# Attention in a fused two-layer trunk: both reciprocals of a unit stand behind the unit's last row minimum on VectorE, the normalisations on GpSimd follow them

## The chip, the cores and the metric

The kernel runs on one core of one Trainium2 chip. The metric is the device time of one launch in microseconds (us); lower is better. Engines are named as in the profile: PE is TensorE (PEld its weight loads), DVE is VectorE, ACT is ScalarE, POOL is GpSimd, SP is SyncE, whose queue issues the DMAs.

## The reference

Two layers over a sequence of 1024 tokens and width 1024, all in float32. Each layer has a token mixer and a SwiGLU feed-forward part, both normalised and modulated by a conditioning vector. Layer 0 mixes with forgetting attention (16 heads of 64), layer 1 with gated linear attention. The change touches the attention of layer 0 alone:

```python
proj = h @ w_in
q, k, v, f_logit = jnp.split(proj, [D_MODEL, 2 * D_MODEL, 3 * D_MODEL], axis=-1)
log_f = jax.nn.log_sigmoid(f_logit + b_f)
cum = jnp.cumsum(log_f, axis=1)
for blk in range(S // Q_BLOCK):                       # 8 blocks of 128 queries
    logits = einsum('bqhd,bkhd->bhqk', q[:, qs:qe], k[:, :qe]) * scale
    logits = logits + cum[:, :, qs:qe, None] - cum[:, :, None, :qe]
    p = softmax(where(causal mask, logits, -inf))
    outs.append(einsum('bhqk,bkhd->bqhd', p, v[:, :qe]))
return concatenate(outs) @ w_out
```

## The kernel before

Products are made in three matmuls of high and low parts, so that two 32-bit reduced operands give nearly a float32 result: `mm3` (lines 317, 318, 319) issues high by high, high by low, low by high. Every such operand has to be split first: ACT casts the high part, DVE or POOL subtracts it from the source (`split`, lines 175 and 176, and the same for weights at 243 and 247).

Attention goes by pairs of heads, `p` = 0 to 7, each with two heads `a`. A head has four units, `g`, worked on in the order 0, 3, 1, 2. A unit `(p, a, g)` is two rows of scores, `qi` = 0 and 1: query blocks `qb` = 2g and 2g+1, of (qb+1) x 128 keys. There are 64 units and 128 rows. For each row

- PE makes the scores in one or two tiles of up to 512 keys (tiles `s...`, lines 1348, 1350, and for some diagonal tiles a mask by 1352). The tiles take turns in two PSUM banks, b0 and b1, so a tile cannot be started before DVE has read the tile two before it.
- DVE takes the row minimum of the negated scores with the forgetting terms added (`tensor_tensor_reduce`, line 1356), from PSUM into the row's buffer `lp`. This is what frees the PSUM bank.
- ACT makes the exponential in place and its sum (line 1360).
- DVE makes the reciprocal of the sum, a 128x1 operation (line 1361).
- POOL multiplies the row by it in place (line 1362).

`outputs(u, lps)` then transposes the normalised rows on PE (tiles `t...`, line 1382, three PSUM banks), splits them on ACT and DVE into `pt`, multiplies them by the values on PE (tiles `o...`, lines 1394 and 1396, one PSUM bank), and adds the halves of that bank on ACT (1411) and DVE (1412) into `oT`. In the program it comes behind the scores of the next unit.

While the attention of pair p runs, PE also projects queries and keys for pair p+1 (tiles `qk...`) and values (tiles `vps...`); these take turns in two other PSUM banks, b6 and b7. A tile of queries is read by two ACT operations and then by two DVE operations of line 896 and 898 (`QA`, `QB`), 64x512 each. `weave` interleaves the two streams by estimated costs and lets the projections run ahead of the attention by at most 18 steps.

What stands on each engine's queue is settled when the kernel is built: a scheduler walks through the program with a timeline of its own estimates and puts, on each engine, the instruction that it takes to be ready. A queue is then strictly in order on the chip. `issue_after`, `in_order` and `behind_one` add constraints of order alone between instructions of one engine: `behind_one(e, at)` puts every instruction of engine `e` that is written in its block behind the instruction `at`, and `last_of(e)` is the last one written so far for `e`. In the program of before, the reciprocal and the normalisation of a row are written right behind its exponential, ahead of the next row's scores.

Of the kernel before, what the change touches and what calls it, by code (L numbers as in the profile page):

```python
# [14 lines left out]
ALU = mybir.AluOpType  # L15
# [3 lines left out]
D = 1024  # L19
# [34 lines left out]
def trunk(ctx, tc, x, c, ada_w, ada_b, norm1_g, norm2_g, ffn_w_in, ffn_w_out,  # L54
          fox_w_in, fox_b_f, fox_w_out, gla_w_in, gla_w_a2, gla_b_a, gla_g_o,
          gla_w_out, final_g, out, dbg=None, stop=None):
    nc = tc.nc
# [51 lines left out]
    def psl(t, n=1):  # L109
        return slice(t * P, (t + n) * P)  # L110
# [145 lines left out]
    @contextmanager  # L256
    def behind_one(e, at):

        bb = nc.cur_bb.bb.instructions
        n = len(bb)  # L260
        yield
        for i in bb[n:]:
            if i.engine == ENG[e]:
                tc.add_manual_dep(i, at.name, mybir.DependencyInfo(
                    mybir.DependencyClass.NoSync, mybir.DependencyReason.DATA), reason="order")
# [36 lines left out]
    class Weights:  # L302
# [7 lines left out]
        def next(self):  # L310
            while self.loads and len(self.got) < self.depth:
                f, *a = self.loads.popleft()
                self.got.append(f(*a))
            return self.got.popleft()
# [133 lines left out]
    def last_of(e):  # L448
        return next(i for i in reversed(nc.cur_bb.bb.instructions) if i.engine == ENG[e])
# [877 lines left out]
    def scores(u):  # L1327

        p, a, g = u
        t = qkt[p]  # L1330
        Qs, K1, KL = (t["QA"], t["KA"], t["KLA"]) if a == 0 else (t["QB"], t["KB"], t["KLB"])
        cm = cums[2 * p + a]
        own = {0: near_t[:, 0:P], 1: near_t[:, P:], 4: far_t[:, 0:2 * P], 5: far_t[:, 2 * P:]}
        if g < 2:
            both = lpr([P, (4 * g + 3) * P], F32, f"lp{p}{a}{g}")
            lps = [both[:, 0:(2 * g + 1) * P], both[:, (2 * g + 1) * P:]]
        else:
            lps = [lpr([P, (2 * g + 1 + i) * P], F32, f"lp{p}{a}{g}{i}") for i in range(2)]
        st = sm.tile([P, 2, 4], F32, tag="st", bufs=4, name=f"st{p}{a}{g}")
        for qi in range(2):  # L1340
            qb = 2 * g + qi
            qs, lp, Wd, mcur = psl(qb), lps[qi], (qb + 1) * P, 3e38
            cuts = (0, 384, 640) if Wd == 640 else (0, Wd) if Wd <= HALF else (0, HALF, Wd)
            for n_, (k0, k1) in enumerate(zip(cuts, cuts[1:])):
                ps = sr([P, k1 - k0], F32, f"s{p}{a}{qb}{k0}")
                early = u == (0, 0, 0)
                diag = k1 == Wd
                nc.tensor.matmul(ps, Qs[:, qs], K1[:, k0:k1], start=True, stop=False)
                by_pe = diag and qb in (2, 3, 6)
                nc.tensor.matmul(ps, Qs[:, qs], KL[:, k0:k1], start=False, stop=not by_pe)  # L1350
                if by_pe:
                    nc.tensor.matmul(ps[:, k1 - k0 - P:], identb, maskb, start=False, stop=True)
                mnew = st[:, qi, n_:n_ + 1]
                cmk = own[qb] if diag and qb in own else cm[:, k0:k1]
                with tc.issue_after(v_last) if early else ExitStack():
                    nc.vector.tensor_tensor_reduce(lp[:, k0:k1], ps, cmk, 1.0, mcur,  # L1356
                                                   ALU.add, ALU.min, mnew)
                mcur = mnew
                yield max(0.22, 0.00085 * (k1 - k0))
            nc.scalar.activation(lp, lp, AF.Exp, bias=mcur, scale=-1.0, accum_out=st[:, qi, 2:3])  # L1360
            nc.vector.reciprocal(st[:, qi, 3:4], st[:, qi, 2:3])  # L1361
            nc.gpsimd.tensor_scalar(lp, lp, st[:, qi, 3:4], 1.0, op0=ALU.mult, op1=ALU.mult)  # L1362
        return lps

    def outputs(u, lps):
# [60 lines left out]
    def attention(p):  # L1426
        for a in range(2):
            h = 2 * p + a
            for i, g in enumerate(ORDER):
                u = (p, a, g)  # L1430
                if h and i == 1:
                    mask_far()
                lps = yield from scores(u)
                if i == 0:
                    if h:
                        mask_last(h)
                    load_near(h + 1)
                elif i == 1:
                    mask_near(h + 1)
                elif i == 3:  # L1440
                    load_far(h + 1)
                    load_cum(h + 2)
                if p:
                    if p > 0:
                        ada0(0.4)
                    ada0p(0.8)
                if pending[0] is not None:
                    yield from finish(*pending[0])
                pending[0] = (u, lps)
        if p == 7:  # L1450
            yield from finish(*pending[0])
# [1197 lines left out]
```

## Time and profile before

| | |
|---|---|
| three runs | 2345.64 us median, 2344.7 to 2349.95 |
| the profiled execution | 2345.56 us, of which the span of the core's work is 2343.8 |
| attention | about 98 to 592 us of the span |
| PE busy | 2322.6 us, 99% of the span |
| DVE, POOL, ACT busy | 1772.7 us (76%), 1160.5 us (50%), 1128.0 us (48%) |
| L1361, reciprocals | 128, 163 ns each |
| L1362, normalisations | 128, 775 ns each in the mean |
| mean granted TensorE clock | 0.997 |

PE is the busiest engine by far. But a matmul's busy time covers its latency, and a following one overlaps it: matmuls of 512 columns that follow each other start about 0.23 us apart and last 0.39 us each. So a stall of less than some 0.15 us is not seen as idle time, and a longer one is seen shortened by about that. Starts of matmuls, one after the other, tell more than the busy share.

### The profile page before, as it was taken

The page shows a single profiled execution, that of the slowest core. Times are in us where ns is not written, and L with a number is a line of the kernel's source. Part 1 is how long each engine was busy: PE and PEld are TensorE (multiplying, and loading weights), DVE is VectorE, ACT ScalarE, POOL GpSimd, SP SyncE. Part 2 cuts the span into 40 slices and gives each one's busy share as a digit, 9 for nine tenths or more (in the row PEclk, how much of TensorE's full clock was granted, in tenths as well). Part 3 has the DMA queues.
Part 4 walks back from the last instruction along what each step waited for, and adds up shares of the span by engine and source line. Part 5 has one row for each costly group of instructions (what it writes and reads, how often), then busy time and mean ns, then how long its engine had stood idle before and what let it go on. Part 6 is the DMA issues. An engine that isn't in the chain of part 4 may idle for free.

```text
span 2343.8 us, 35552 instructions
## 1 busy us (share of the span) xinstructions
PE 2322.6 (99%) x12088; PEld 1980.6 (85%) x12088; DVE 1772.7 (76%) x2946; ACT 1128.0 (48%) x2166; POOL 1160.5 (50%) x1027
## 2 busy tenths in 40 slices
PE   8999999999999999999999999999999999999999
PEld 7988888888888888788888899898888888888888
DVE  6577677776788888997888666668787777876787
ACT  6566566675544333334325654345444333345236
POOL 1345454533446656665563522345456666664651
PEclk9999999999999999999999999999999999999999
DMA  8533343352435545459774443555434544458674
GB/s 259 163 99 112 109 120 107 113 169 84 153 100 175 187 158 176 154 203 315 267 265 155 136 128 99 151 171 172 150 102 162 174 147 159 141 189 300 237 264 141
DMA packets 359342, 390.72 MB, mean 167 GB/s; under 512 B 26908, under 2 KB 296376, under 8 KB 359160
## 3 DMA queue, kind: packets, MB, share of 16 engines
q1 hardware_dynamic: 359160, 388.45, 50.7%
q8 instruction: 95, 1.56, 0.3%
q14 instruction: 87, 0.71, 0.1%
HBM read 287.10 MB, written 101.25 MB: 166 GB/s over the span
## 4 chain that ended last, share of the span: by engine, by line
PE 54%; DVE 4%; DMA 3%; POOL 2%; issue 2%; SPq 0%; ACT 0%; POOLq 0%; DVEq 0%; ACTq 0%
PE p_b L317 11%; PE p_b L319 11%; PE p_b L318 11%; PE gv_b L317 1%; PE gv_b L319 1%; PE gv_b L318 1%; PE gr_b L317 1%; PE gr_b L319 1%; PE gr_b L318 1%; DVE o_s L176 1%; DVE ad_s L543 1%; DMA ex_s<-x_sp 1%; PE gqp_b L317 0%; PE gk_b L317 0%; PE f1a_b L319 0%
## 5 line engine op out<-in xcount | busy, mean ns | idle before, releaser
L175 ACT CAST o_s<-xv_s 128x512 fp32r<-128x512 f32 (+1 forms) x392 | 235.9, 610 | 328.4 <-PE p_b L319 218.5
L176 DVE TENSOR_TENSOR o_s<-xv_s,o_s 128x512 fp32r<-128x512 f32 (+1 forms) x392 | 332.7, 854 | 37.2 <-ACT o_s L175 36.3
L317 PE MATMUL p_b<-B,o_s 128*128 128x512 f32 x608 | 235.4, 391 | 0.9 <-DVE ex_s L1745 0.5
L318 PE MATMUL p_b<-B,o_s 128*128 128x512 f32 x608 | 236.1, 389 | 0.0
L319 PE MATMUL p_b<-B,o_s 128*128 128x512 f32 x608 | 235.1, 389 | 0.0
L978 POOL TENSOR_TENSOR ex_s<-xv_s,xv_s 128x512 f32<-128x512 f32 (+1 forms) x64 | 96.0, 1499 | 238.8 <-DMA xv_s<-in_ffn_w_in_dram 123.3
L1362 POOL TENSOR_SCALAR lp_s<-lp_s,st 128x128 f32<-128x128 f32 (+7 forms) x128 | 98.9, 775 | 220.9 <-DVE st L1361 191.8
L317 PE MATMUL p_b<-T,o_s 128*128 128x512 f32 x480 | 186.7, 390 | 1.8 <-DVE x L1745 1.8
L318 PE MATMUL p_b<-T,o_s 128*128 128x512 f32 x480 | 186.7, 389 | 0.0
L319 PE MATMUL p_b<-T,o_s 128*128 128x512 f32 x480 | 181.2, 389 | 0.0
L1360 ACT ACTIVATE lp_s<-lp_s,st 128x128 f32<-128x128 f32 (+7 forms) x128 | 99.5, 777 | 85.4 <-DVE st L1356 68.1
L317 PEld LDWEIGHTS p_b<-B,o_s 128*128 128x128 f32 x608 | 114.1, 188 | 26.6 <-issue 1.6
L319 PEld LDWEIGHTS p_b<-B,o_s 128*128 128x128 f32 x608 | 114.1, 188 | 23.9
L318 PEld LDWEIGHTS p_b<-B,o_s 128*128 128x128 f32 x608 | 114.2, 188 | 23.2
L980 POOL TENSOR_TENSOR xv_s<-ex_s,xv_s 128x512 f32<-128x512 f32 (+1 forms) x64 | 95.7, 1495 | 51.2 <-DVE o_s L176 47.9
L1745 DVE TENSOR_TENSOR ex_s<-ex_s,p_b 128x512 f32<-128x512 f32 x140 | 94.2, 680 | 29.9 <-PE p_b L319 29.6
L990 POOL TENSOR_TENSOR xv_s<-xv_s,xv_s 128x512 f32<-128x512 f32 x48 | 65.8, 1370 | 97.9 <-issue 54.7
L176 DVE TENSOR_TENSOR pt_s<-t_b,pt_s 128x512 fp32r<-128x512 f32 (+1 forms) x160 | 98.4, 632 | 20.3 <-ACT pt_s L175 19.1
L317 PEld LDWEIGHTS p_b<-T,o_s 128*128 128x128 f32 x480 | 90.1, 188 | 21.3 <-DVE x L1745 2.2
L175 ACT CAST pt_s<-t_b 128x512 fp32r<-128x512 f32 (+1 forms) x160 | 82.6, 544 | 51.1 <-PE t_b L1382 32.6
L319 PEld LDWEIGHTS p_b<-T,o_s 128*128 128x128 f32 x480 | 90.1, 188 | 18.7
L318 PEld LDWEIGHTS p_b<-T,o_s 128*128 128x128 f32 x480 | 90.1, 188 | 18.6
(1539 smaller groups left out, 7378.2 us busy)
## 6 DMA issues: line engine op xcount, KB each, us to landing
xv_s<-in_ffn_w_in_dram SPq DMA_DIRECT2D x176, 256.0 KB, 3.2
hid_B<-x SPq DMA_DIRECT2D x66, 512.0 KB, 3.0
ad_s<-in_ada_w_dram SPq DMA_DIRECT2D x384, 64.0 KB, 2.4
hid_T<-x SPq DMA_DIRECT2D x44, 512.0 KB, 2.9
xv_s<-in_ffn_w_out_dram SPq DMA_DIRECT2D x88, 256.0 KB, 3.6
T2o<-hid_T SPq DMA_DIRECT2D x22, 512.0 KB, 7.0
T1o<-hid_T SPq DMA_DIRECT2D x22, 512.0 KB, 6.2
B11o<-hid_B SPq DMA_DIRECT2D x22, 512.0 KB, 5.9
```

Of the source, the lines that this page charges most:

```text
L175: nc.scalar.copy(hi, src)
L176: nc.vector.tensor_sub(lo, src, hi.bitcast(F32))
L317: nc.tensor.matmul(ps, ah, bh, start=start, stop=False, skip_group_check=chain)
L318: nc.tensor.matmul(ps, ah, bl, start=False, stop=False, skip_group_check=chain)
L319: nc.tensor.matmul(ps, al, bh, start=False, stop=stop, skip_group_check=chain)
L543: nc.vector.scalar_tensor_tensor(acc, raw[:, t], c42[:, o:o + 1], acc, op0=ALU.mult, op1=ALU.add)
L978: nc.gpsimd.tensor_add(s1, a21, a22)
L980: nc.gpsimd.tensor_sub(a11, s1, a11)
L990: nc.gpsimd.tensor_sub(r[A12], r[A12], r[A11])
L1360: nc.scalar.activation(lp, lp, AF.Exp, bias=mcur, scale=-1.0, accum_out=st[:, qi, 2:3])
L1362: nc.gpsimd.tensor_scalar(lp, lp, st[:, qi, 3:4], 1.0, op0=ALU.mult, op1=ALU.mult)
L1745: nc.vector.tensor_add(d, d if src is None else dest(G, src), ps)
```

## The change

The reciprocals and the normalisations of both rows are written behind the loop over the rows, that is behind the exponential of the second row, and the reciprocals are held on DVE behind the last row minimum of the unit.

```diff
             nc.scalar.activation(lp, lp, AF.Exp, bias=mcur, scale=-1.0, accum_out=st[:, qi, 2:3])
-            nc.vector.reciprocal(st[:, qi, 3:4], st[:, qi, 2:3])
-            nc.gpsimd.tensor_scalar(lp, lp, st[:, qi, 3:4], 1.0, op0=ALU.mult, op1=ALU.mult)
+        at = last_of("D")
+        for qi in range(2):
+            with behind_one("D", at):
+                nc.vector.reciprocal(st[:, qi, 3:4], st[:, qi, 2:3])
+            nc.gpsimd.tensor_scalar(lps[qi], lps[qi], st[:, qi, 3:4], 1.0, op0=ALU.mult, op1=ALU.mult)
         return lps
```

Every instruction is kept, none is added. Lines behind the change move by three (1361 becomes 1364, 1362 becomes 1365, 1382 becomes 1385, 1396 becomes 1399). Because the scheduler settles all queues anew, the order within attention changes on every engine, on PE too; from the end of attention on all queues stand as before. In the rows below a name carries p, a, and then g for a row buffer (`lp2030`: p 2, a 0, g 3, row 0) or qb and the first key for a score tile (`s207512`: p 2, a 0, qb 7, keys from 512); `b0` or `b1` behind it is the PSUM bank.

PE in the unit (2, 0, 3) and the next one, where the profile of before has its longest waits. Before:

```order
L1348 MATMUL s207512_b1_54_2582<-KA2_1686,QA2_1684 128x512
L1350 MATMUL s207512_b1_54_2582<-KLA_201,QA2_1684 128x512
L1382 MATMUL t2000_b3_41_2606<-ident_67,lp200_s48_28_2451 128x128 x3
L1348 MATMUL s2020_b0_55_2627<-KA2_1686,QA2_1684 128x384
L1350 MATMUL s2020_b0_55_2627<-KLA_201,QA2_1684 128x384
L1352 LDWEIGHTS identb_72
L1352 MATMUL s2020_b0_55_2627<-maskb_84,identb_72 128x128
L1348 MATMUL s2030_b1_56_2638<-KA2_1686,QA2_1684 128x512
L1350 MATMUL s2030_b1_56_2638<-KLA_201,QA2_1684 128x512
L1352 LDWEIGHTS identb_72
L1352 MATMUL s2030_b1_56_2638<-maskb_84,identb_72 128x128
L1348 MATMUL s2040_b0_57_2763<-KA2_1686,QA2_1684 128x384
```

The same place of the program on PE after the change:

```order
L1348 MATMUL s2070_b0_53_2576<-KA2_1686,QA2_1684 128x512
L1350 MATMUL s2070_b0_53_2576<-KLA_201,QA2_1684 128x512
L319 MATMUL qk031_b7_18_2571<-h0h7_189,w384_l_s24_18_1936 128x512
L317 MATMUL vps20_b6_19_2708<-wv2560_0h_s19_19_2193,h0h0_175 128x256
L318 MATMUL vps20_b6_19_2708<-wv2560_0l_s20_20_2194,h0h0_175 128x256
L319 MATMUL vps20_b6_19_2708<-wv2560_0h_s19_19_2193,h0l0_176 128x256
L317 MATMUL vps20_b6_19_2708<-wv2560_0h_s19_19_2193,h0h1_177 128x256
L318 MATMUL vps20_b6_19_2708<-wv2560_0l_s20_20_2194,h0h1_177 128x256
L319 MATMUL vps20_b6_19_2708<-wv2560_0h_s19_19_2193,h0l1_178 128x256
L1348 MATMUL s207512_b1_54_2580<-KA2_1686,QA2_1684 128x512
L1350 MATMUL s207512_b1_54_2580<-KLA_201,QA2_1684 128x512
L1399 MATMUL o112_b5_16_2494<-pt1120_s50_38_2500,v00_s27_1_797 128x256 x4
```

Before, five score tiles stood in a row with three transposes between them; after, each is set apart by projections or products with the values (`s2020` comes ten rows behind the last row shown, `s2030` much later).

PE in the unit (5, 0, 3). Before:

```order
L1348 MATMUL s5070_b0_125_4879<-KA5_3990,QA5_3988 128x512
L1350 MATMUL s5070_b0_125_4879<-KLA_201,QA5_3988 128x512
L319 MATMUL vps32_b7_38_5015<-wv2816_0h_s19_43_4489,h0l1_178 128x256
L1396 MATMUL o412_b5_40_4795<-pt4120_s50_98_4801,v20_s27_9_2829 128x256
L1348 MATMUL s507512_b1_126_4883<-KA5_3990,QA5_3988 128x512
L1350 MATMUL s507512_b1_126_4883<-KLA_201,QA5_3988 128x512
L1396 MATMUL o412_b5_40_4795<-pt4120_s50_98_4801,v20_s27_9_2829 128x256 x3
L1396 MATMUL o412_b5_40_4795<-pt4121_s51_99_4812,v21_s28_10_2953 128x256
L1382 MATMUL t5000_b3_101_4902<-ident_67,lp500_s48_64_4747 128x128 x3
L317 MATMUL vps32_b7_38_5015<-wv2816_0h_s19_43_4489,h0h2_179 128x256
```

The same place on PE after the change; ahead of these rows stand, from the last matmul of the query tile `qk061` on, three matmuls of `vps32`, the two of `s506512`, eight of `o411`, the mask of `s506512` and one matmul of `vps32`:

```order
L1348 MATMUL s5070_b0_125_4877<-KA5_3990,QA5_3988 128x512
L1350 MATMUL s5070_b0_125_4877<-KLA_201,QA5_3988 128x512
L318 MATMUL vps32_b7_38_5015<-wv2816_0l_s20_44_4490,h0h1_177 128x256
L319 MATMUL vps32_b7_38_5015<-wv2816_0h_s19_43_4489,h0l1_178 128x256
L1385 MATMUL t5000_b3_101_4902<-ident_67,lp500_s48_64_4747 128x128 x3
L1348 MATMUL s507512_b1_126_4881<-KA5_3990,QA5_3988 128x512
L1350 MATMUL s507512_b1_126_4881<-KLA_201,QA5_3988 128x512
L1348 MATMUL s5020_b0_127_4923<-KA5_3990,QA5_3988 128x384
L1350 MATMUL s5020_b0_127_4923<-KLA_201,QA5_3988 128x384
L1352 LDWEIGHTS identb_72
L1352 MATMUL s5020_b0_127_4923<-maskb_84,identb_72 128x128
L1399 MATMUL o412_b5_40_4795<-pt4120_s50_98_4801,v20_s27_9_2829 128x256 x4
```

Here the score tile `s5020`, which needs the bank of `s5070`, has moved up to stand right behind `s507512`, and `o412` behind it.

DVE at that place, from the minimum of `s506512` on. Before:

```order
L1356 ISA lp5030_s45_65_4853,st503_4855<-s506512_b1_124_4863,cum10_s43_11_4330,st503_4855 128x384
L1356 ISA st503_4855 128x1
L176 TENSOR_TENSOR pt4120_s50_98_4801<-t4120_b3_98_4796,pt4120_s50_98_4801 128x512
L176 TENSOR_TENSOR pt4121_s51_99_4812<-t4121_b4_99_4807,pt4121_s51_99_4812 128x512
L176 TENSOR_TENSOR pt4122_s49_100_4822<-t4122_b2_100_4818,pt4122_s49_100_4822 128x384
L1356 ISA lp5031_s46_66_4854,st503_4855<-s5070_b0_125_4879,cum10_s43_11_4330 128x512
L1356 ISA st503_4855 128x1
L1361 RECIPROCAL st503_4855<-st503_4855 128x1
L1356 ISA lp5031_s46_66_4854,st503_4855<-s507512_b1_126_4883,cum10_s43_11_4330,st503_4855 128x512
L1356 ISA st503_4855 128x1
L247 TENSOR_TENSOR w1792_l_s24_48_4998<-w1792__s16_43_4995,w1792_h_s23_47_4997 128x256
L896 SCALAR_TENSOR_TENSOR QA6_4753<-qk061_b6_37_4872,QA6_4753 64x512
```

After:

```order
L1356 ISA lp5030_s45_65_4853,st503_4855<-s506512_b1_124_4863,cum10_s43_11_4330,st503_4855 128x384
L1356 ISA st503_4855 128x1
L896 SCALAR_TENSOR_TENSOR QA6_4753<-qk061_b6_37_4872,QA6_4753 64x512
L898 SCALAR_TENSOR_TENSOR QB6_4754<-qk061_b6_37_4872,QB6_4754 64x512
L1356 ISA lp5031_s46_66_4854,st503_4855<-s5070_b0_125_4877,cum10_s43_11_4330 128x512
L1356 ISA st503_4855 128x1
L176 TENSOR_TENSOR pt4121_s51_99_4812<-t4121_b4_99_4807,pt4121_s51_99_4812 128x512
L1415 TENSOR_TENSOR oT4_s52_5_4129<-o411_b5_39_4721,oT4_s52_5_4129 64x256
L176 TENSOR_TENSOR pt4122_s49_100_4822<-t4122_b2_100_4818,pt4122_s49_100_4822 128x384
L1356 ISA lp5031_s46_66_4854,st503_4855<-s507512_b1_126_4881,cum10_s43_11_4330,st503_4855 128x512
L1356 ISA st503_4855 128x1
L1364 RECIPROCAL st503_4855<-st503_4855 128x1
```

The reciprocal of the first row (L1361, now L1364) has gone from between the minima of `s5070` and `s507512` to behind the latter, as the change asks in every unit; and the reading of the query tile (`QA6`, `QB6`) has come to stand ahead of the minimum of `s5070`.

## The prediction

> **What bounds the kernel now.** I read the page first, then the sums by stage, then PE's waits in attention, then the timeline at each place where PE waited.
>
> ```profile
> span 2343.8 us, 35552 instructions
> 220.00:280.00 60.00, 58.28 (x379) 51.68 (x379) 40.63 (x111) 38.24 (x82) 32.60 (x48) 0.97 0.36 109
> 280.00:340.00 60.00, 58.91 (x395) 52.87 (x394) 44.38 (x116) 38.12 (x81) 31.04 (x44) 1.00 0.35 108
> 592.00:800.00 208.00, 207.96 (x943) 172.69 (x942) 170.66 (x234) 93.92 (x159) 111.79 (x79) 1.00 0.48 156
> ```
>
> The columns of a stage are its length, then busy time (and count) of PE, PEld, DVE, ACT and POOL, the granted clock, and the DMA. PE is busy for nearly all of every stage, DVE for two thirds of it. So DVE is not the bound, and the change can only be worth what PE loses inside attention, 98 to 592 us. The stage behind attention has no idle PE (207.96 of 208 us) and an unchanged order: what attention gains or loses arrives at the end in full.
>
> ```profile
> PE s_b L1348 <- DVE st L1356: 1.5, 2, 1.2
> PE t_b L1382 <- POOL lp_s L1362: 1.0, 1, 1.0
> ...
> PE mp_b L460 <- DVE QB L898: 0.6, 1, 0.6
> ```
>
> ```profile
>   ACT lp_s L1360: 31.6, 50
> ...
>   POOL lp_s L1362: 191.8, 78
> ```
>
> The first fence is PE's waits within attention (total, times, longest): a score tile waited for a row minimum, a transpose for a normalisation, each once or twice. The second is the reciprocal of line 1361: DVE stood 31.6 us, in 50 waits, for the exponential, and POOL stood 191.8 us for DVE. Large numbers, but hardly any of it reaches PE.
>
> The places where it does, in order of time: place A, PE and DVE, unit (2, 0, 3) and the next.
>
> ```profile
> 231.31 0.49 PE L1382 MATMUL t_b<-ident,lp_s 128*128 128x128 f32 x3
> 231.91 0.44 PE L1348 MATMUL s_b<-KA,QA 128*128 128x384 f32 x1
> 232.11 0.74 DVE L1356 CUSTOM_DVE_ANT_0 lp_s<-s_b,cum_s,st 128x512 f32<-128x512 f32 x1
> 232.37 0.23 PE L1352 MATMUL s_b<-maskb,identb 128*128 128x128 bf16 x1
> 232.89 0.68 DVE L896 SCALAR_TENSOR_TENSOR QA<-qk_b,QA 64x512 fp32r<-64x512 f32 x1
> 232.92 0.50 PE L1348 MATMUL s_b<-KA,QA 128*128 128x512 f32 x1 [0.32 <-DVE st L1356]
> 233.49 0.23 PE L1352 MATMUL s_b<-maskb,identb 128*128 128x128 bf16 x1
> 233.59 0.69 DVE L898 SCALAR_TENSOR_TENSOR QB<-qk_b,QB 64x512 fp32r<-64x512 f32 x1
> 234.31 0.56 DVE L1356 CUSTOM_DVE_ANT_0 lp_s<-s_b,cum_s 128x384 f32<-128x384 f32 x1
> 234.93 0.44 PE L1348 MATMUL s_b<-KA,QA 128*128 128x384 f32 x1 [1.21 <-DVE st L1356]
> 235.22 0.34 PE L1350 MATMUL s_b<-KLA,QA 128*128 128x384 f32 x1
> 235.63 0.38 PE L1382 MATMUL t_b<-ident,lp_s 128*128 128x128 f32 x1
> 236.00 2.29 PE L1396 MATMUL o_b<-pt_s,v_s 128*128 128x256 f32 x9
> ```
>
> ```profile
> 235.00:236.00 1.00, 0.92 (x4) 0.37 (x4) 0.94 (x3) 0.68 (x2) 0.35 (x1) 0.87 0.95 337
> 236.00:239.00 3.00, 3.00 (x15) 3.00 (x15) 2.47 (x9) 1.19 (x3) 1.69 (x2) 0.50 0.01 2
> 239.00:240.00 1.00, 1.00 (x10) 1.00 (x10) 0.00 (x0) 0.00 (x0) 1.00 (x3) 0.93 0.00 0
> ```
>
> Place B, a few units later (PE, and QB on DVE):
>
> ```profile
> 295.67 0.40 PE L1350 MATMUL s_b<-KLA,QA 128*128 128x512 f32 x1
> 295.92 0.69 DVE L898 SCALAR_TENSOR_TENSOR QB<-qk_b,QB 64x512 fp32r<-64x512 f32 x1
> 296.67 0.61 PE L460 MATMUL mp_b<-four,acc_s 128*128 128x4 f32 x4 [0.60 <-DVE QB L898]
> ...
> 297.86 0.23 PE L1352 MATMUL s_b<-maskb,identb 128*128 128x128 bf16 x1
> ...
> 298.46 0.74 PE L1396 MATMUL o_b<-pt_s,v_s 128*128 128x256 f32 x4 [0.37 <-DVE oT_s L1412]
> ```
>
> Rows for pricing the new order, from the place called E below as it ran before, and from a reciprocal that waited and its normalisation:
>
> ```profile
> 415.33 0.62 DVE L1356 CUSTOM_DVE_ANT_0 lp_s<-s_b,cum_s,st 128x384 f32<-128x384 f32 x1
> 417.14 0.40 PE L1350 MATMUL s_b<-KLA,QA 128*128 128x512 f32 x1
> 417.37 0.28 PE L319 MATMUL vps_b<-wv_0h_s,h0l 128*128 128x256 f32 x1
> 417.49 0.28 PE L1396 MATMUL o_b<-pt_s,v_s 128*128 128x256 f32 x1
> 417.61 0.40 PE L1348 MATMUL s_b<-KA,QA 128*128 128x512 f32 x1
> 417.68 0.69 DVE L1356 CUSTOM_DVE_ANT_0 lp_s<-s_b,cum_s 128x512 f32<-128x512 f32 x1
> ...
> 228.85 0.69 DVE L176 TENSOR_TENSOR pt_s<-t_b,pt_s 128x512 fp32r<-128x512 f32 x1
> ...
> 414.87 0.43 DVE L1412 TENSOR_TENSOR oT_s<-o_b,oT_s 64x256 f32<-64x256 f32 x1 [0.40 <-ACT oT_s L1411]
> ...
> 230.40 0.16 DVE L1361 RECIPROCAL st<-st 128x1 f32<-128x1 f32 x1 [0.86 <-ACT lp_s L1360]
> ...
> 230.90 1.01 POOL L1362 TENSOR_SCALAR lp_s<-lp_s,st 128x896 f32<-128x896 f32 x1
> ```
>
> From start to start, matmuls of 512 columns take 0.23 us (417.14 to 417.37) and of 256 columns 0.12; I take 0.18 for 384 between these, and 0.11 for a transpose (three in 0.49, of which one latency). Those are PE's real costs; the longer durations overlap.
>
> **The change part by part.** No instruction comes or goes, so no engine's work changes. Three things move.
>
> *DVE's waits for the exponential.* The first row's reciprocal now stands behind the second row's minima, when its exponential is long done. I cost this at nothing by itself: PE's list has no wait that ends on line 1361. The second row's reciprocal still has to wait for the exponential that follows the last minimum. Behind a waiting reciprocal on DVE stand minima and splits; they get earlier, and that is cover for what comes below.
>
> *The first row's normalisation and transposes.* Reciprocal and POOL's multiplication start behind the last minimum instead of behind the first row's exponential. On POOL's queue the multiplication falls behind weight splits and adaLN products that stood after it; no wait of PE ends on those. On SP no transfer belongs to the moved step; loads of the forgetting terms wait for row minima, which do not get later by it, and no matmul in attention waits for a load. PE's order follows: the first row's transposes stand later too. From the last score matmul to the first transpose the new queue has 2.3 us of PE work at the closest unit, (7, 1, 3), and 3.7 at the next. Needed are: latency and start 0.25, minimum 0.69, its accumulator 0.08, reciprocal 0.16, 0.34 from its end to POOL's start (230.56 to 230.90), multiplication 1.01: 2.5 us. So 0.3 us of wait at one unit, and cover of over 1 us at all others: **+0.3**.
>
> *PE's order of score tiles.* A score tile needs the bank of the tile two before it. PE work between that tile's last matmul and this one's first, summed over the queue by the costs above, is the cover for the minimum. Before, the five shortest of 190 are 0.6 to 1.1 us (`s2040`, `s706512`, `s2030`, `s2020`, `s307512`); a minimum alone takes 0.25 + 0.7. After, none is under 1.2.
>
> Place A goes. Its waits, start to start less the cost: 0.27 at `s2020` (231.31 to 231.91), 0.49 at `s2030` (mask at 232.37, next 232.92, 0.06 for the mask), 1.38 at `s2040` (233.49 to 234.93), 0.23 and 0.26 at the two steps behind (235.22 to 235.63 to 236.00), since DVE's backlog reached the splits: 2.6 us. And the granted clock fell to 0.50 behind it: 1 us at 0.87, 3 at 0.50, 1 at 0.93 lose 0.13 + 1.5 + 0.07 = 1.7 us. Together **-4.3**. In the new queue these three have 3.4 to 3.7 us of PE work as cover, against 0.6 to 1.0.
>
> Place B goes as well: in the new queue the `mp` product comes some 60 rows later, `s3020` has projections ahead of it, and `o212` stands far from `o211`. Its cost: 0.77 (295.67 to 296.67, less 0.23) + 0.37 at `s3020` + 0.54 (297.86 to 298.46, less 0.06) = 1.7. The middle one is the rest of the same backlog, taken at the size of its neighbour's shown idle time. **-1.7**.
>
> Place E is new: unit (5, 0, 3). Count from the start of the last `qk061` matmul. PE: 0.23, three `vps` 0.36, `s506512` 0.36, eight `o411` 0.95, mask: its result stands at about 2.1. DVE: minimum of `s506512` 0.62 + 0.08 to 2.8; QA and QB, which now stand ahead, 0.68 + 0.69 to 4.15; minimum of `s5070` 0.69 to 4.85. PE meanwhile: mask and `vps` to 2.05, `s5070` 0.46, `vps` 0.24, transposes 0.33, `s507512` 0.46: at 3.5 it stands before `s5020`, which needs the bank of `s5070`: a wait of 1.4. Then `s5020` and its mask, 0.45, and `o412` at 5.35 needs the one `o` bank, freed by oT of `o411`, which on DVE stands behind a split: 4.93 + 0.69 + 0.43 = 6.05: a wait of 0.7. **+2.1**. It is place A's pattern on a smaller scale: QA and QB in front of a minimum.
>
> Waits that I leave as they are: those around 468, 485 and 500 to 520 us, where the new order is nearly the old.
>
> Sum: -4.3 - 1.7 + 2.1 + 0.3 = -3.6 us, on the profiled execution's 2345.56 (span 2343.8 and 1.8 around it; 0.08 under the median of the runs, 2345.64): **2342.0 us**, 0.15% faster. What a measurement of this kernel tells from no change is about 0.2%, 4.7 us, so the forecast counts as the same.
>
> [...]
>
> **The rivals.**
>
> *E does not bite, and the gain is larger.* If ACT and DVE run ahead at E by what the reciprocals no longer hold up (one wait cost DVE 0.86), the minimum of `s5070` is in time. For it: the 31.6 us of such waits; against: what delays it is work, not a wait. Then -4.3 - 1.7 + 0.3 = -5.7: 2339.9, faster by 0.24%.
>
> *The clock drops at E.* Its 2.1 us of waits within 2.6 us are close to A's 2.6 within 4.5. Then +1.7: 2343.7, the same.
>
> *Slower: POOL comes late for the first row.* In the new queue the closest seven units have 2.3, 3.7, 4.1, 4.1, 4.2, 4.4 and 4.6 us of PE work ahead of the first transposes. If POOL is busy with other rows when the reciprocal is done, so that the chain takes 5.1 us rather than 2.5, PE waits 2.8 + 1.4 + 1.0 + 1.0 + 0.9 + 0.7 + 0.5 = 8.3, of which 0.3 is counted: 2342.0 + 8.0 = 2350.0. It decides from a chain of about 4.5 on. For it: before, PE did wait for POOL once, 1.0 us. Against: POOL is half idle.
>
> *Nothing reaches PE.* A and B go, but other bunches of like size that I have not seen come: 2345.6. For it: the waits are set by a scheduler that knew nothing of them; against: the distances, of which the shortest have grown.
>
> **How the numbers follow.** Forecast 0.36; E harmless 0.31; clock drop at E 0.17; other bunches 0.09; POOL late 0.07. Faster by over 0.2%: the second case and nothing else, 0.31. Slower: POOL late, and 0.01 of the bunches, 0.08. Same: 0.61. The range of 8 in 10 reaches from E harmless with 0.5 us of small waits gone, 2339.4, to the clock drop with about 1.5 more of bunches, 2345.2.
>
> **What the profile will show.** Right: no wait of PE for line 1356 around 231 to 235 us and no stage at 0.97 clock there; the wait for `mp` gone; one wait of PE of over 1 us for a minimum near 415 us with QA and QB ahead of it on DVE; DVE's wait for the exponential about halved from 31.6. Wrong: a clock under 1.00 in 400 to 460; new waits of PE for POOL's line 1365; a gain spread over all of attention rather than at two places.

## The result, and the profile after

The changed kernel took 2342.72 us (median of 12 runs, 2338.45 to 2346.55), the kernel before 2345.97 in the runs beside them (12, 2344.35 to 2351.16). The ratio is 0.9981, with a 95% interval of 0.9973 to 0.9989: 0.19% faster. That is 4.5 us, the difference of the means; the medians are 3.25 us apart. It is clear of no change, and just under the 0.2% from which the prediction counts a kernel as faster. The forecast was 2342.0. One run of the experiment e2 below took 8960.03 us and is left out of its ratio, not of its median; all other runs of this study took 2334 to 2353 us. The profiled execution took 2340.03 us, its span is 2338.3.

The stages of the changed kernel that answer to those of before (columns as there), and PE's waits within attention:

```profile
220.00:280.00 60.00, 60.00 (x401) 53.74 (x400) 44.14 (x116) 38.76 (x84) 33.87 (x49) 1.00 0.36 112
280.00:340.00 60.00, 59.90 (x399) 53.75 (x398) 44.86 (x120) 38.48 (x83) 32.75 (x48) 1.00 0.40 115
400.00:460.00 60.00, 58.43 (x395) 52.61 (x394) 44.15 (x119) 39.75 (x85) 33.55 (x49) 1.00 0.34 106
```

```profile
PE s_b L1348 <- DVE st L1356: 1.8, 3, 1.2
PE qk_b L317 <- DVE QB L898: 0.7, 1, 0.7
PE o_b L1399 <- DVE oT_s L1415: 0.4, 1, 0.4
```

The first stage (place A) has no idle PE left, and its granted clock is 1.00 instead of 0.97. The second (place B) has 0.1 us of idle PE instead of 1.1. The third, which holds place E, has 1.6 us. In the list the `mp` product no longer waits for QB, and no transpose waits for POOL. The score tiles still wait 1.8 us in all; before it was 1.5, but at other places. The reciprocal, now line 1364:

```profile
  ACT lp_s L1360: 11.5, 26
  POOL lp_s L1365: 170.2, 82
```

DVE's wait for the exponential fell from 31.6 to 11.5 us, a third rather than a half.

Place E in the changed kernel, PE and DVE in order of time:

```profile
408.82 0.39 PE L1348 MATMUL s_b<-KA,QA 128*128 128x512 f32 x1
408.85 0.62 DVE L1356 CUSTOM_DVE_ANT_0 lp_s<-s_b,cum_s,st 128x384 f32<-128x384 f32 x1 [0.30 <-PE s_b L1352]
409.05 0.40 PE L1350 MATMUL s_b<-KLA,QA 128*128 128x512 f32 x1
409.51 0.68 DVE L896 SCALAR_TENSOR_TENSOR QA<-qk_b,QA 64x512 fp32r<-64x512 f32 x1
410.09 0.40 PE L1350 MATMUL s_b<-KLA,QA 128*128 128x512 f32 x1
410.21 0.69 DVE L898 SCALAR_TENSOR_TENSOR QB<-qk_b,QB 64x512 fp32r<-64x512 f32 x1
410.93 0.69 DVE L1356 CUSTOM_DVE_ANT_0 lp_s<-s_b,cum_s 128x512 f32<-128x512 f32 x1
411.69 0.44 PE L1348 MATMUL s_b<-KA,QA 128*128 128x384 f32 x1 [1.20 <-DVE st L1356]
412.14 0.23 PE L1352 MATMUL s_b<-maskb,identb 128*128 128x128 bf16 x1
412.27 0.43 DVE L1415 TENSOR_TENSOR oT_s<-o_b,oT_s 64x256 f32<-64x256 f32 x1
412.75 1.33 PE L1399 MATMUL o_b<-pt_s,v_s 128*128 128x256 f32 x9 [0.37 <-DVE oT_s L1415]
```

The score tile of 408.82 (`s5070`) is complete at 409.45, but its minimum starts on DVE at 410.93, because QA and QB stand ahead of it. `s5020` needs that bank and starts at 411.69, 1.6 us after the matmul before it (410.09), where 0.23 is the cost: a wait of 1.37 us. Behind it `o412` waits for oT: 412.75 less 412.14, less the 0.04 of a mask (408.58 to 408.62 at the one before), another 0.57. Together 1.9 us, and 2.1 with the small ones around it, as priced.

Attention alone can be read more sharply than the whole run. I take the time from its first score matmul to the first matmul of the feed-forward part. Before:

```profile
98.30 0.22 PE L1348 MATMUL s_b<-KA,QA 128*128 128x128 f32 x1
635.23 0.62 PE L317 MATMUL p_b<-B,o_s 128*128 128x512 f32 x2
```

After:

```profile
95.61 0.22 PE L1348 MATMUL s_b<-KA,QA 128*128 128x128 f32 x1
627.77 0.61 PE L317 MATMUL p_b<-B,o_s 128*128 128x512 f32 x2
```

That is 536.9 us before and 532.2 after: 4.8 us less. The rest of the span isn't the change's: 2.7 us came from the start (98.30 against 95.61), whose program stands as it was, and 2.0 were lost behind attention (1708.6 against 1710.6), whose order stands as it was too (the last difference on PE is at 614 us of before). Over the ten traces of this study the start takes 95.4 to 98.7 us and the part behind attention 1708.6 to 1713.8. So one profile's span says little about 4 us, while the attention stage repeats well, as the first experiment shows.

### The profile page after: what moved, and what is told of

The parts are those of the page before. It is cut to its first block, busy times and chain, and to the rows that moved or that the text cites. A ratio compares the mean times of both kernels' runs of the same rounds, so it can differ in the third digit from the quotient of the medians.

```text
span 2338.3 us, 35579 instructions
## 1 busy us (share of the span) xinstructions
PE 2316.1 (99%) x12088; PEld 1975.4 (84%) x12088; DVE 1774.2 (76%) x2946; ACT 1125.1 (48%) x2166; POOL 1160.4 (50%) x1027
## 4 chain that ended last, share of the span: by engine, by line
PE 58%; DVE 3%; DMA 2%; issue 1%; POOL 1%; SPq 0%; ACT 0%; POOLq 0%; DVEq 0%; ACTq 0%
PE p_b L317 12%; PE p_b L318 12%; PE p_b L319 12%; PE gv_b L317 1%; PE gv_b L319 1%; PE gv_b L318 1%; PE gr_b L317 1%; PE gr_b L319 1%; PE gr_b L318 1%; PE gqp_b L319 1%; PE gk_b L317 1%; PE gqp_b L317 1%; PE gk_b L319 1%; PE gk_b L318 1%; PE gqp_b L318 1%
## 5 line engine op out<-in xcount | busy, mean ns | idle before, releaser
L247 POOL TENSOR_TENSOR w_l_s<-w__s,w_h_s 128x256 fp32r<-128x256 f32 x90 | 69.9, 804 | 81.3 <-ACT w_h_s L243 80.5
L317 PEld LDWEIGHTS p_b<-T,o_s 128*128 128x128 f32 x480 | 90.1, 188 | 20.9 <-DVE x L1748 1.9
L319 PEld LDWEIGHTS p_b<-T,o_s 128*128 128x128 f32 x480 | 90.1, 188 | 18.8
```

The costliest lines, as they stand in the source:

```text
L247: (nc.gpsimd if i < 3 else nc.vector).tensor_sub(lo[:, cs], rw[:, cs], hi[:, cs].bitcast(F32))
L317: nc.tensor.matmul(ps, ah, bh, start=start, stop=False, skip_group_check=chain)
L319: nc.tensor.matmul(ps, al, bh, start=False, stop=stop, skip_group_check=chain)
```

## The experiments

All eight, with the attention stage as just defined. The kernel before was run again beside each set, and each ratio is to the runs beside it; e4 has six runs, f3 five, the others eleven:

| kernel | median, us | ratio to before, 95% interval | attention, us |
|---|---|---|---|
| before | 2345.97 (changed), 2347.36 (e1 to e4), 2346.25 (f1 to f4) | 1 | 536.9 |
| changed | 2342.72 | 0.9981 [0.9973, 0.9989] | 532.2 |
| e1, changed again | 2342.61 | 0.9981 [0.9972, 0.9990] | 532.2 |
| e2, source moved, no hold | 2346.99 | 0.9995 [0.9985, 1.0004] | 537.2 |
| e3, before, QA and QB late at A and B | 2342.02 | 0.9982 [0.9973, 0.9991] | 533.2 |
| e4, changed, QA and QB late at E | 2339.37 | 0.9972 [0.9961, 0.9984] | 530.3 |
| f1, hold in pairs 0 to 4 | 2340.89 | 0.9977 [0.9968, 0.9986] | 531.7 |
| f2, hold in pairs 5 to 7 | 2343.86 | 0.9988 [0.9979, 0.9997] | 535.3 |
| f3, changed, lag 20 | 2338.42 | 0.9959 [0.9945, 0.9974] | 528.2 |
| f4, before, lag 20 | 2341.78 | 0.9981 [0.9972, 0.9990] | 530.5 |

The theory: the change acts only through the order of the queues. It matters where QA and QB (or other work) stand on DVE ahead of a minimum whose bank PE needs soon, and nowhere else. The rival: DVE's shorter waits for the exponential are a gain in themselves, in every unit.

**e1: the changed kernel again.**

> The changed kernel once more, on another chip perhaps. From the first score matmul to the first feed-forward matmul on PE the profile of before has 536.9 us and that of the change 532.2. My theory (the order of PE and DVE at places A, B and E makes the whole difference, and order is fixed at build time): again 532.2 within 0.5, with one wait of PE of about 1.2 us for a row minimum near 412 us and none around 231; the whole kernel 2 to 5 us under before. Rival (the difference is noise of the chip, since the stages outside attention differed by 2.7 us at the start too): this stretch anywhere from 531 to 537.

532.2 us again, and the same bunch at 410 us. On all engines the instructions come in the same order as in the first trace of the changed kernel, and the stage repeats within 0.1 us.

**e2: the move in the source without the hold.**

```diff
-            with behind_one("D", at):
-                nc.vector.reciprocal(st[:, qi, 3:4], st[:, qi, 2:3])
+            nc.vector.reciprocal(st[:, qi, 3:4], st[:, qi, 2:3])
```

> Reciprocals and normalisations written behind both rows, but without the hold on VectorE behind the last minimum; all results the same. Theory (the hold is what moves the first row's reciprocal, and with it the order on PE): places A and B stay as before, PE waits of 2 to 3 us for row minima around 231 to 235 and the clock at 0.50 behind them, 536.9 +- 0.7 us from the first score matmul to the first feed-forward matmul, total within 1.5 us of before. Rival (moving the normalisations in the source suffices): 532.2.

PE's waits within attention in this kernel:

```profile
PE s_b L1348 <- DVE st L1356: 1.5, 2, 1.2
PE t_b L1384 <- POOL lp_s L1364: 1.0, 1, 1.0
PE qk_b L317 <- DVE QB L898: 0.7, 1, 0.7
PE mp_b L460 <- DVE QB L898: 0.6, 1, 0.6
...
```

They are those of before, and so is the time. In the two traces PE, DVE, ACT and POOL take the same instructions in the same order: written later, the reciprocals are put back behind their exponentials by the scheduler. The hold is the whole change. So e2 is also a repeat of before, and the 537.2 us against 536.9 show how far the stage of one and the same order can vary.

**e3: the kernel before, with QA and QB taken out of the way at A and B.**

```diff
 # qk_proj, on the kernel before
-            (k_evac if i else q_evac)(ps, qkt[p], hf)
+            with behind_one("D", last_of("D")) if (p, i, hf) in {(3, 0, 1), (4, 0, 1)} else ExitStack():
+                (k_evac if i else q_evac)(ps, qkt[p], hf)
```

> The kernel before, with the last reading of the query tile (QA, QB on VectorE) of pairs 3 and 4 held behind what is written ahead of it, so that it no longer stands in front of the row minima at places A and B; the order of score tiles at A on PE stays as it was. Theory (1.4 us of QA and QB in front of a minimum is one half of the wait at A, the bunched tiles the other): the wait at s2040 falls from 1.38 to about 0.4, no drop of the clock, B's waits gone; 532.5 to 534 us from the first score matmul to the first feed-forward matmul. Rival (the bunched score tiles alone do it, DVE's queue does not matter): A keeps over 2 us of waits and the drop of the clock, 535 to 536.

The stage of place A, PE's waits, and the reciprocal's wait in this kernel:

```profile
220.00:280.00 60.00, 59.51 (x398) 52.83 (x397) 44.71 (x120) 40.56 (x87) 33.15 (x48) 1.00 0.37 112
```

```profile
PE t_b L1383 <- POOL lp_s L1363: 1.0, 1, 1.0
PE fo011p_b L317 <- DVE x L1517: 0.9, 1, 0.9
PE qk_b L317 <- DVE QB L898: 0.7, 1, 0.7
PE s_b L1349 <- DVE st L1357: 0.3, 1, 0.3
```

```profile
  ACT lp_s L1361: 31.5, 47
```

Nothing of the change is in this kernel, and the reciprocals still wait 31.5 us. Yet A shrank to some 1.5 us without a drop of the clock, B is gone, and 3.7 us of attention with them, although a projection `fo011p` now waits 0.9 us near 515. At A the experiment is clean: from 218 to 242 us of before PE has the same order in both kernels, and what DVE has ahead of the late minimum differs only in QA and QB, which now come 11 us behind it. So it is shown that QA and QB in front of a row minimum make 2.9 us of A, the drop of the clock included; the rest stays, with the bunched score tiles. At B the order on PE is another too (the `mp` product comes at 304 us instead of 297), so that B has the same cause is read from the trace of before and not shown by itself. And since the reciprocals wait as long as before, the gain doesn't come from shorter waits.

**e4: the changed kernel, with QA and QB taken out of the way at E.** The same edit on the changed kernel, for `(6, 0, 1)` alone.

> The changed kernel with the last reading of the query tile of pair 6 held in the same way, so that QA and QB no longer stand in front of the minimum of s5070 at place E. Theory: the wait at E, 2.1 us, goes; the order behind it shifts, and two tiles in the last pair come closer (cover 0.85 and 1.2 us), up to 0.5 us; 530.1 to 530.7 from the first score matmul to the first feed-forward matmul, total 1.5 to 2 us under the changed kernel. Rival (E's wait comes from the late second transposes and ACT, not from QA and QB): 532.

The same score tiles as above, in this kernel:

```profile
411.18 0.69 DVE L1357 CUSTOM_DVE_ANT_0 lp_s<-s_b,cum_s 128x512 f32<-128x512 f32 x1
411.67 0.40 PE L1351 MATMUL s_b<-KLA,QA 128*128 128x512 f32 x1
411.94 0.44 PE L1349 MATMUL s_b<-KA,QA 128*128 128x384 f32 x1
```

The minimum starts ahead of QA and QB, and the tile that needs its bank follows 0.27 us after the matmul before it, against 1.6. Attention took 530.3 us, 1.9 less. Around E the order on PE is the changed kernel's, and on DVE only QA and QB have moved (to 424.87), so the 1.3 us that are gone there are shown to be theirs; `o412` still waits. The rest of the 1.9 us is made elsewhere, by small waits that come (0.7 us near 424) and go (0.9 near 500) with the new order. That the time fell into the expected 530.1 to 530.7 is luck in part.

**f1 and f2: the hold in the pairs 0 to 4 alone, and in the pairs 5 to 7 alone.**

```diff
-            with behind_one("D", at):
+            with behind_one("D", at) if p < 5 else ExitStack():     # f1; f2: p >= 5
```

> The changed kernel, with the hold on the reciprocal kept for the head pairs 0 to 4 and dropped for pairs 5 to 7 (both reciprocals stay behind the second row's exponential in the source). PE's queue is the changed kernel's up to just behind s5020, so the waits at 231 to 235 us and at 294 to 298 us should be gone and the new bunch near 410 us (minimum of s5070 behind QA and QB) should be there. From the first score matmul to the first feed-forward matmul the kernel before took 536.9 us and the changed one 532.2. Theory (the hold acts only through the order of the queues, place by place): 532.0 to 534.0, the upper end if the wait for POOL at 468 us and the small one near 485 come back; about 0.15% faster than before. Rival (the hold pays in every unit, by DVE's shorter waits for the exponential): five eighths of 4.7, so 534.0.

> The changed kernel, with the hold dropped for the head pairs 0 to 4 and kept for pairs 5 to 7. PE's queue is the kernel before's up to 410 us, so the waits at 231 to 235 us with the half clock and those at 294 to 298 us should be there, and no bunch near 410. Theory: 535.0 to 537.0 us from the first score matmul to the first feed-forward matmul (536.9 before), the lower end if the wait for POOL at 468 us (1.9 us) stays away as it does in the changed kernel; the same time as before within 0.1%. Rival (the hold pays in every unit): three eighths of 4.7, so 535.1, without any change of the waits at 231 to 298. The gains of this run and of the one with pairs 0 to 4 should add up to about the changed kernel's 4.7.

The stages of A and of E, in f1 and then in f2:

```profile
220.00:280.00 60.00, 60.00 (x399) 53.78 (x398) 44.13 (x115) 38.18 (x82) 33.35 (x48) 1.00 0.38 117
400.00:460.00 60.00, 58.43 (x396) 52.60 (x395) 42.60 (x116) 39.12 (x85) 32.87 (x48) 1.00 0.33 104
```

```profile
220.00:280.00 60.00, 58.21 (x369) 51.31 (x368) 40.14 (x111) 37.71 (x81) 32.64 (x48) 0.97 0.36 109
400.00:460.00 60.00, 60.00 (x398) 53.82 (x397) 43.02 (x119) 38.84 (x84) 32.86 (x48) 1.00 0.36 114
```

f1 has no A and has E; f2 has A, with its drop of the clock, and no E. The times are 531.7 and 535.3: gains of 5.2 and 1.6. For f1 the theory's 532.0 to 534.0 was a little too slow and the rival's 534.0 more so. For f2 the two expected nearly the same, and only the places speak: the waits of A and B stand there, as the theory had it. The gains add up to 6.8 rather than to 4.7. Most of the difference is the wait for POOL near 468 us (place C below): of its 1.9 us all goes in f1 and 1.5 in f2, and so most of it is counted twice.

**f3 and f4: another order altogether, with the hold and without.**

```diff
-    LAGS = dict(P=18)
+    LAGS = dict(P=20)
```

> The changed kernel, with the one number that sets how far PE's filler work may lag behind the score tiles raised from 18 to 20. It leaves out nothing. The order changes over all of attention. Theory (what counts is the PE work that stands between a score tile and the tile two before it, and what DVE has queued ahead of its minimum): the shortest covers are 1.20 (s606512), 1.23 (s6020), 1.24 (s7020) and 1.8 us, with QA and QB ahead of no minimum at these; no bunch near 410: 529.5 to 531.0 us from the first score matmul to the first feed-forward matmul, about 0.25% faster than before. Rival (the order near 410 has nothing to do with it, the rest is general): 532.2 as the changed kernel.

> The kernel before (reciprocal right behind its own exponential, no hold), with the same number raised from 18 to 20. The order changes over all of attention, the reciprocals keep waiting for their exponentials on DVE. Theory (only the order of the queues counts): the shortest cover of a score tile is 0.73 us (s6060), then 1.33 and 1.6, against 0.64, 0.69, 1.0, 1.0 and 1.1 before: one wait of about 0.5 us at s6060, none at the old places: 530.0 to 532.0 us from the first score matmul to the first feed-forward matmul, about 0.25% faster than before without the change. Rival (the change's gain is DVE's shorter wait for the exponential): 537, no gain, since those waits stay at about 30 us.

PE's waits in f3; and in f4, with the reciprocal's wait on DVE:

```profile
PE s_b L1348 <- DVE st L1356: 0.5, 1, 0.5
PE qk_b L317 <- DVE QB L898: 0.3, 1, 0.3
```

```profile
PE qk_b L317 <- DVE QB L898: 1.6, 2, 0.9
PE qk_b L317 <- DVE KLB L911: 1.0, 1, 1.0
```

```profile
  ACT lp_s L1360: 27.8, 47
```

f4 has no hold and DVE waits 27.8 us for exponentials, yet attention takes 530.5, less than in the changed kernel. So the gain can be had, and more, with hardly shorter waits. Beside f3, which has the hold, f4 is 2.3 us longer; 1.8 of these are PE's waits in the lists above, 2.6 against 0.8, and the rest isn't assigned. The place was missed, though: `s6060` didn't wait, and instead PE's projections waited 2.6 us for their banks, read by QA, QB and by KLA, KLB, at three places. Score tiles aren't the only ones to be covered. f3 is the fastest kernel of the study: 528.2 us of attention, 0.41% faster than before (five runs), and 4 us of attention less than the change alone. It went past its expectation of 529.5 to 531.0.

## Why the prediction was right, step by step

Its time holds (2342.0 against 2342.72), but its sum of -3.6 against the measured -4.8 of attention is a balance of terms that held, one step that didn't, and waits that it had not foreseen. I lay the two traces side by side at equal points of PE's work, with each matmul counted at the median distance from its start to the next (0.23 us for 512 columns, 0.18 for 384, 0.12 for 256, 0.11 for a transpose, 0.04 for a mask), and take by how much the starts fell behind that in each stretch:

| step | forecast | measured |
|---|---|---|
| A goes, with its drop of the clock | -4.3 | -4.6 |
| B goes | -1.7 | -1.7 |
| E is new | +2.1 | +2.0 |
| first row's normalisation late at (7, 1, 3) | +0.3 | no wait for POOL is left |
| 468, 485, 500 to 520 "as they are" | 0 | -1.9, +0.5, -0.2 |
| waits not foreseen, near 214 and 301 us of the changed kernel | 0 | +1.0 |

The rows measured add up to -4.9; the 0.1 to -4.8 is rounding. What the prediction left out came to -1.6 and to +1.0, which partly cancel, and the median of the kernel before differs by 1.7 us from set to set, so that the forecast came within 0.7 us of the measured time is luck in part.

Between the places next to nothing happens. From 242 to 284 and from 315 to 414 us of before, more than a quarter of attention, the changed kernel gains 0.2 us in all, where a gain alike in every unit would be over 1.2. That speaks against the rival of the experiments by the two traces alone.

The clock stayed at 1.00 around E, so the rival of a drop there fell; E cost what was forecast, so "E harmless" fell; no transpose waits for POOL, so "POOL comes late" fell; other bunches came to +1.0 us, not to the 3.6 that would have eaten the gain. e3, e4 and f4 show that it is order that pays.

The step that failed is "Waits that I leave as they are". I took the new order for nearly the old one there, because PE's rows read alike, and didn't compare what DVE and POOL do ahead of it. The wait of a transpose for POOL at 468 us, place C, went away:

```profile
440.79 0.39 PE L1348 MATMUL s_b<-KB,QB 128*128 128x512 f32 x1
441.90 2.49 SPq L454 DMA_DIRECT2D ada_s<-in_ada_w_dram  x4
446.64 0.48 DVE L543 SCALAR_TENSOR_TENSOR acc_s<-ada_s,c,acc_s 128x256 f32<-128x256 f32 x1 [2.56 <-DMA ada_s<-in_ada_w_dram]
469.88 1.09 PE L1382 MATMUL t_b<-ident,lp_s 128*128 128x128 f32 x8 [1.00 <-POOL lp_s L1362]
```

```profile
434.77 2.49 SPq L454 DMA_DIRECT2D ada_s<-in_ada_w_dram  x4
434.86 0.40 PE L1348 MATMUL s_b<-KB,QB 128*128 128x512 f32 x1
439.41 2.05 DVE L543 SCALAR_TENSOR_TENSOR acc_s<-ada_s,c,acc_s 128x256 f32<-128x256 f32 x4 [2.16 <-DMA ada_s<-in_ada_w_dram]
```

The first fence is the kernel before, the second the changed one, at the same score tile. An adaLN load leaves SP 1.1 us behind the start of that tile before, and 0.1 ahead of it after. DVE's products of line 543, which wait for the load, start 5.9 us behind the tile before and 4.6 after. Until 464 us the row minima of before then start 2.1 to 4.3 us behind the last matmul of their tiles, at the same tiles of the changed kernel 0.1 to 1.8, and at 468 the transpose waits. In the eight traces with the old lag, the later the load left, the longer the wait:

| kernel | load behind the tile, us | wait near 468, us |
|---|---|---|
| e2 | 1.4 | 2.1 |
| before | 1.1 | 1.9 |
| e3 | 0.75 | 1.4 |
| f2 | 0.6 | 0.4 |
| e4 | 0.6 | under 0.3 |
| changed, e1, f1 | -0.1 | under 0.3 |

Where the hold stands does not decide it: f1 has none in the pairs 5 to 7 and no wait, f2 has it and keeps 0.4 (at a projection just behind the transposes). Nearest to an experiment are before and e2, whose order is the same on every engine: the load left 0.3 us later in e2, and the wait was 0.2 longer. That is one pair and a small difference, and no run moves the load alone, so this chain is read from traces and not shown.

"What attention gains or loses arrives at the end in full" holds within what the runs can tell: against the 4.8 us of attention the means of the changed kernel gained 4.5, and its repeat gained 4.75 in the median. f4 is the worst case, with 6.4 us in attention and 4.5 in the median. In a single trace it doesn't hold, for the part behind attention varies by 5 us, as said above.

## What to carry to other kernels

Where PE bounds a kernel at 99%, look for the few places where its queue waits, and for what stands on the other engine ahead of the instruction that frees the bank; a long wait on an engine that isn't the bound (here 31.5 us) may be worth nothing. Reordering pays or costs place by place, so an edit that moves a whole stage is best priced by comparing the queues of all engines, not of PE alone, at every place with a wait and at every new bunch; here what the comparison left out was worth 1.6 us one way and 1.0 the other. To measure a few microseconds in a kernel of 2340, take the stage between two fixed instructions out of the trace, and let the runs confirm it.

## What the hardware showed beyond that

The granted clock didn't go by the sum of nearby waits, as my rival for E had it. A place far behind attention, near 1200 us, shows it. f2 and then f4, PE's waits and the stage around them:

```profile
1203.66 0.50 PE L317 MATMUL f0a_b<-B11o,o_s 128*128 128x512 f32 x1 [0.49 <-ACT o_s L175]
1205.57 0.50 PE L319 MATMUL f0a_b<-B11o,o_s 128*128 128x512 f32 x1 [1.18 <-DVE o_s L176]
1195.00:1225.00 30.00, 28.33 (x118) 22.67 (x118) 25.59 (x36) 10.41 (x19) 15.93 (x12) 0.94 0.99 350
```

```profile
1201.92 0.50 PE L317 MATMUL f0a_b<-B11o,o_s 128*128 128x512 f32 x1 [0.94 <-ACT o_s L175]
1204.15 0.50 PE L319 MATMUL f0a_b<-B11o,o_s 128*128 128x512 f32 x1 [1.49 <-DVE o_s L176]
1195.00:1225.00 30.00, 27.50 (x121) 21.85 (x120) 24.91 (x37) 10.40 (x19) 15.97 (x12) 1.00 0.95 332
```

In f2 the two waits are 1.67 us together, and the clock of the stage is 0.94; in f4 they are 2.43, and it is 1.00. At A in the kernel before, waits of 0.32 and 1.21 us stand ahead of 3 us at a clock of 0.50; at E in the changed kernel there are waits of 1.20 and 0.37, and the clock from 405 to 420 us is 1.00. The kernel before also has a single wait of 1.76 us, up to 947.75, and a clock of 1.00 from 940 to 950. So the clock fell behind waits of at most 1.21 us at A and 1.18 in f2, and stayed up behind a longer one: neither the longest wait nor the sum of nearby ones tells by itself whether it falls. What does is not shown by these runs, so that E would keep its clock could not be read from its waits; the measurement decided it.
